# A hybrid attention and convolution layer: later weights are split on GpSimd in the middle of a pair of heads, and a row's maximum is carried from its first part into its second

## The chip, the cores and the metric

The kernel runs on one core of a Trainium2 chip. It uses TensorE (PE, matrix products and transposes), VectorE (DVE), ScalarE (ACT), GpSimd (POOL) and the DMA queue of SyncE (SP). The time is device microseconds of the whole program; smaller is better. A profile is one execution with every instruction's start and duration on record.

## The reference, cut to what matters

One layer: an RMS-normalised, modulated input goes through one projection, which feeds a convolution module and grouped-query attention; both are gated, joined and projected out. The change lies in the attention and in the preparation of weights that are used behind it.

```python
def attend_blocked(q, k, v):          # 8 query heads, 2 key heads, 1024 latent queries,
    ...                               # 1024 latent + 256 context keys
    s = jnp.einsum('bqkgd,bskd->bkgqs', qblk, k).astype(jnp.float32) * scale
    pr = jax.nn.softmax(s, axis=-1).astype(v.dtype)
    return jnp.einsum('bkgqs,bskd->bqkgd', pr, v)
...
conv = conformer_conv(...) * silu(...)            # ends in: y @ w_pw + b_pw
out = jnp.concatenate([attn, conv], axis=-1) @ w_out[l]
```

The softmax subtracts each row's maximum over all 1280 keys. The matrix products are done in two parts each (a rounded high part `hi` and the rest `lo`), so every weight and every tile of probabilities is split once: `hi` is a rounded copy, `lo` is the source less `hi`.

## The kernel before, in words

The program has three stages: the projection with the convolution (to about 306 us of the span), the attention (to about 550 us), and a tail with the layer norm, the pointwise product and the output projection.

In the attention the work comes in 32 units (group `g` of 256 queries, head `h`), taken two at a time as 16 pairs. A unit has two tiles of 128 queries (`t`) and five blocks of 256 keys (`k`). Its steps are named by two letters, the unit of the pair and the tile or block: `qa`, `qb` are the score products into PSUM (1024 keys and 256 keys); `ma`, `mb`, `mc` make the negated maximum of a row (over the first 1024 keys, over the other 256, and the smaller of both); `ex` is the exponential on ScalarE, which takes that maximum as its bias; `tr` turns a block on TensorE into one of two PSUM banks `pt`; `ra`, `hi`, `lo` split it; `pv` multiplies by the values; `rz`, `gs`, `ol`, `ad`, `gt`, `mu`, `mh`, `ml` normalise, gate and split the result. `MODE = "DRRRD"` says how a block is split: blocks 0 and 4 have `hi` on ScalarE and `lo` on VectorE, both straight from PSUM; blocks 1 to 3 are first copied to SBUF by ScalarE (`ra`), then `hi` is a VectorE cast from SBUF to SBUF (L700) and `lo` a GpSimd subtraction (L706). The bank `pt` is free again when `lo` (blocks 0, 4) or `ra` (blocks 1 to 3) has read it.

The order is written out by hand: `ORDER` gives each step a place in time, repeated every `PERIOD` = 13.4 for the 16 pairs, and every engine takes its steps in that order. Steps with a place over 13.4 run beside later pairs. Folded into one period, VectorE's order is `hi13 hi01 hi02 ma00 mb00 rz0 mc00 rz1 lo04 lo10 ma01 mb01 mc01 hi11 ad1 hi12 mu hi03 ma10 mb10 mc10 lo14 lo00 ma11 mb11 mc11 ad0`, and GpSimd's is `lo13 lo01 gs1 lo02 gs0 lo03 ml lo11 lo12`.

Other work is hung into the same order by `hooks`. Four weight tiles for the tail (`wo0`, `wo1`, `wp0`, `wp1`) are fetched by DMA (`stage`) and split a half at a time (`split`, 128x512 each), one half in each of the pairs 8 to 15, at place 0 of the pair, that is behind `ad0` and ahead of `hi13`. Before the change both parts of a split are VectorE's: a cast (L114) and a subtraction (L116). In pairs 0 to 13 `q_turn` transposes queries for later units (L609) at place 4, into a bank of the same two as `pt`.

Of the kernel before, what the change touches and what calls it, by code (L numbers as in the profile page):

```python
# [11 lines left out]
BF16 = mybir.dt.bfloat16  # L12
AF = mybir.ActivationFunctionType
ALU = mybir.AluOpType
AX = mybir.AxisListType
# [3 lines left out]
P = 128  # L19
# [5 lines left out]
KEYS = S + CTX  # L25
# [5 lines left out]


ORDER = {
# [13 lines left out]
PERIOD = 13.4  # L47
# [19 lines left out]
OA = 23.31, 25.5, 31.35  # L67

WP = 8

MODF = 3
TLO = ['dp', 'pp', 'pp', 'dd', 'dd', 'dd', 'pd', 'dd']
# [8 lines left out]
class Layer:  # L81
# [27 lines left out]
    def split(self, hi, lo, src, hi_on="act", lo_on="dve"):  # L109
        nc = self.nc  # L110
        if hi_on == "act":
            nc.scalar.activation(hi, src, AF.Copy)
        else:
            nc.vector.tensor_copy(out=hi, in_=src)  # L114
        eng = nc.gpsimd if lo_on[0] == "p" else nc.vector
        eng.tensor_sub(out=lo, in0=src, in1=hi.bitcast(F32))  # L116

# [532 lines left out]

    def op_ma(self, u, t):
        st = self.st[u]
        st["nm", t] = nm = self.small([P, 3], "nm", "nm")
        r = self.nc.vector.reduce_max(out=nm[:, 0:1], in_=self.s5[:, 1536 * t:1536 * t + 1024], axis=AX.X, negate=True)  # L654
        self.s_deps("DVE", r, [st["q", t, 0]])

    def op_mb(self, u, t):
        st = self.st[u]
        r = self.nc.vector.reduce_max(out=st["nm", t][:, 1:2], in_=self.s5[:, 1024 + 256 * t:1280 + 256 * t],  # L659
                                      axis=AX.X, negate=True)  # L660
        self.s_deps("DVE", r, [st["q", t, 1]])

    def op_mc(self, u, t):
        nm = self.st[u]["nm", t]
        self.nc.vector.tensor_tensor(out=nm[:, 2:3], in0=nm[:, 0:1], in1=nm[:, 1:2], op=ALU.min)  # L665

    def op_ex(self, u, t):
        nc, st = self.nc, self.st[u]
        if "z" not in st:
            st["z"] = self.small([P, 2], "z", "z")  # L670
        st["e", t] = e = self.e5.tile([P, KEYS], F32, tag="e", name=f"e{u[0]}{u[1]}{t}")
        ex = nc.scalar.activation(e, self.s5[:, t * KEYS:(t + 1) * KEYS], AF.Exp, bias=st["nm", t][:, 2:3],  # L672
                                  accum_out=st["z"][:, t:t + 1])
        self.s_deps("ACT", ex, [st["q", t, 0], st["q", t, 1]])
        self.s_use[t] = ex.ins

    def op_tr(self, u, k):
# [160 lines left out]
    def run(self):  # L838
# [10 lines left out]
        with ExitStack() as ctx:  # L849
# [9 lines left out]
            with ExitStack() as att:  # L859
                ps = att.enter_context(psum("ps", 1))  # L860
                self.s5 = ps.tile([P, 2 * KEYS], F32, tag="s5", name="s5")
                self.pv_bank = lambda u: pv.tile([P, 512], F32, tag="acc", name=f"pv{u[0]}{u[1]}")
                self.s_use = [None, None]
                self.sync_dep = mybir.DependencyInfo(mybir.DependencyClass.Sync, mybir.DependencyReason.DATA)
                hooks = []
                add = lambda t, fn: hooks.append((t, fn))
                acc = {}

                def proj(g, t):
                    if t == 0:  # L870
                        acc[g] = self.bank(QTAG[g], f"q1{g}")
                    self.mm_tok(acc[g], wq, g, t)
                for g in range(1, 4):
                    for t in range(2):
                        add(QP[g - 1][t], lambda g=g, t=t: proj(g, t))
                    add(QN[g - 1], lambda g=g: hl.update({(1, g): self.q(1, g, acc[g].rearrange(
                        "p (t n) -> p t n", t=2))}))
                    add(QS[g - 1], lambda g=g: hl.update({(1, g): self.q_split(1, g, hl[1, g])}))
                for i, (c, g) in enumerate(((1, 0), (0, 1), (1, 1), (0, 2), (1, 2), (0, 3), (1, 3))):
                    for hp in range(2):  # L880
                        add((2 * i + hp) * PERIOD + QT, lambda c=c, g=g, hp=hp: self.q_turn(c, g, hl[c, g], hp))
                st, wt, src = {}, {}, {"wo0": 0, "wo1": 1, "wp0": 0, "wp1": 256}

                def stage(n):
                    if n[1] == "o":
                        st[n] = self.out_stage(0, src[n])
                    else:
                        st[n] = self.w_stage(w_pw, [(src[n], 256)], n, 0)
                    wt[n] = [self.b4(list(st[n].shape), f"{n}{x}", F32R) for x in "hl"]

                def split(n, h):
                    hi, lo, x = (x.rearrange("p a b -> p (a b)")[:, 512 * h:512 * h + 512] for x in (*wt[n], st[n]))
                    self.split(hi, lo, x, hi_on="dve")
                for i, n in enumerate(src):
                    add((WP + 2 * i - 1) * PERIOD, lambda n=n: stage(n))
                    for h in range(2):
                        add((WP + 2 * i + h) * PERIOD, lambda n=n, h=h: split(n, h))
                nw = []

                def tail_pools():  # L900
                    att.close()
                    pools["acc"] = ctx.enter_context(psum("po", 4))
                    pw = ctx.enter_context(psum("pw", 1))
                    self.pw_bank = lambda g, ob: (pw, pv)[ob].tile([P, 512], F32, tag="acc", name=f"pw{g}{ob}")
                    nw.extend([wt["wo0"], wt["wo1"]])
                add(TAIL + CLOSE, tail_pools)
                steps = []
                for g in range(4):
                    steps += [lambda g=g: self.ln_stats(g, 0), lambda g=g: self.ln_stats(g, 1),
                              lambda g=g: self.ln_norm(g), lambda g=g: self.ln_swish(g)]  # L910
                for f, t in zip(steps, LN):
                    add(TAIL + t, f)
                add(TAIL + SILU, lambda: self.nc.scalar.activation(self.small([P, 1], "sj", "sj"), self.ones[:, 0:1],
                                                                   AF.Silu))
                for g, t in enumerate(OA):
                    add(TAIL + t, lambda g=g: self.out_mm(0, g, nw, 0))
                self.attention(hooks)
# [27 lines left out]
    def start(self, w_in):  # L945
# [18 lines left out]
        def scale(i):  # L964
            self.nc.vector.tensor_scalar(out=self.xs[i], in0=self.xs[i], scalar1=r.pop(i), scalar2=None, op0=ALU.mult)
        steps = {"L": self.mod_load, "X": tokens, "W": lambda h: st.update({h: self.w_stage(w_in, wcol, "wglu0", h)}),
                 "S": split, "T": self.mod_split, "C": self.mod_mm, "D": self.mod_cols,
                 "Q": lambda i: r.update({i: self.norm_stats(self.xs[i])}), "R": scale,
                 "P": self.turn_x, "Y": self.tap_rows, "V": self.taps, "U": self.make_u, "M": mm}
# [100 lines left out]
```

## Time and profile before

| | us |
|---|---|
| median of 3 runs (684.4 to 806.51) | 684.53 |
| the profiled execution | 683.55 |
| its span, first to last instruction | 681.7 |
| busy in it: PE / DVE / ACT / POOL | 650.2 / 537.4 / 352.9 / 332.5 |
| mean granted TensorE clock | 0.994 |

Busy time of an engine is the time in which an instruction of it runs. Matmul ends are modelled, so TensorE's busy time overstates its work a little. Idle time of an engine matters only where it holds up the chain that ends last.

### The profile page before, as it was taken

To read this page: it belongs to the slowest core of one execution; us is meant where nothing else is said; L and a number is where in the kernel's file an instruction comes from. 1 tells how busy PE (TensorE), PEld (TensorE's weight loads), DVE (VectorE), ACT (ScalarE), POOL (GpSimd) and SP (SyncE) were. 2 spreads that over 40 slices of the span, in tenths; PEclk is the share of its full clock that TensorE was granted. 3 is DMA by queue.
4 is the path that set the end of the run, shared out by engine and by line. 5 is a ranking of instruction groups with operands and counts; after the bars stand their busy time and mean duration, and the time that the engine had idled before them with its cause. 6 is when DMAs were issued, how large, how long until landed. Compare 5 with 4: busy or idle time off the path is not lost.

```text
span 681.7 us, 11003 instructions
## 1 busy us (share of the span) xinstructions
PE 650.2 (95%) x4258; PEld 572.3 (84%) x4258; DVE 537.4 (79%) x844; ACT 352.9 (52%) x578; POOL 332.5 (49%) x289
## 2 busy tenths in 40 slices
PE   4989999999999999997999999899999999999997
PEld 1467799888888999996899999888888878888885
DVE  2698789749999999876999999999999953545422
ACT  3564325554343122226888888788888845441000
POOL 1244804957329132885656766565566564121200
PEclk9899999999999999999999999999999999999999
DMA  8984310312653232100010001000100021133711
GB/s 266 319 225 129 116 36 1 94 31 62 217 185 124 71 101 78 32 1 1 1 32 1 1 32 60 3 32 25 40 1 1 1 93 32 62 124 132 256 60 46
DMA packets 51251, 53.28 MB, mean 78 GB/s; under 512 B 4521, under 2 KB 41697, under 8 KB 51200
## 3 DMA queue, kind: packets, MB, share of 16 engines
q1 hardware_dynamic: 51104, 52.57, 24.4%
q8 instruction: 33, 0.54, 0.3%
q14 instruction: 18, 0.15, 0.1%
q10 hardware_dynamic: 96, 0.02, 0.0%
HBM read 44.20 MB, written 8.39 MB: 77 GB/s over the span
## 4 chain that ended last, share of the span: by engine, by line
PE 67%; DVE 23%; issue 3%; DMA 3%; ACT 2%; SPq 1%; POOL 0%; DVEq 0%; ACTq 0%
PE o L820 12%; PE pv L715 8%; PE s L636 8%; PE pt L682 7%; DVE y L456 6%; PE g L386 6%; PE a L386 6%; PE kv L412 4%; DVE yp L456 4%; PE pw L531 3%; PE zc L386 3%; PE q L412 3%; DVE p L700 3%; DVE nm L654 2%; DMA wm<-in_w_mod 2%
## 5 line engine op out<-in xcount | busy, mean ns | idle before, releaser
L706 POOL TENSOR_TENSOR p<-raw,p 128x512 fp32r<-128x512 f32 x96 | 127.0, 1337 | 81.2 <-DVE p L700 70.8
L636 PE MATMUL s<-kT,qT 128*128 128x512 f32 (+1 forms) x384 | 100.8, 372 | 4.6 <-ACT e L672 4.5
L715 PE MATMUL pv<-p,v 128*128 128x256 f32 x640 | 103.2, 292 | 0.7 <-DVE mm L747 0.7
L456 DVE SCALAR_TENSOR_TENSOR yp<-up,cw,yp 128x1024 f32<-128x1024 f32 x77 | 99.1, 1287 | 1.9
L682 PE MATMUL pt<-ident,e 128*128 128x128 f32 x640 | 93.5, 273 | 1.0 <-DVE p L706 0.8
L672 ACT ACTIVATE e<-s,nm 128x1280 f32<-128x1280 f32 x64 | 85.0, 1329 | 14.3 <-DVE nm L665 14.1
L715 PEld LDWEIGHTS pv<-p,v 128*128 128x128 f32 x640 | 85.9, 189 | 4.5 <-DVE mm L747 1.5
L654 DVE TENSOR_REDUCE nm<-s 128x1 f32<-128x1024 f32 x64 | 77.7, 1214 | 0.6
L682 PEld LDWEIGHTS pt<-ident,e 128*128 128x128 f32 x640 | 73.3, 141 | 2.6 <-PE pv L715 1.2
L636 PEld LDWEIGHTS s<-kT,qT 128*128 128x128 f32 x384 | 62.7, 189 | 11.6 <-ACT e L672 5.7
L691 ACT ACTIVATE raw<-pt 128x512 f32<-128x512 f32 x96 | 57.5, 600 | 9.6 <-PE pt L682 5.5
L700 DVE CAST p<-raw 128x512 fp32r<-128x512 f32 x96 | 47.3, 520 | 1.8 <-ACT raw L691 1.2
L698 ACT ACTIVATE p<-pt 128x512 fp32r<-128x512 f32 x64 | 38.5, 602 | 11.6 <-PE pt L682 10.3
L706 DVE TENSOR_TENSOR p<-pt,p 128x512 fp32r<-128x512 f32 x64 | 40.9, 676 | 1.4 <-ACT p L698 1.4
L456 DVE SCALAR_TENSOR_TENSOR y<-up,cw,y 128x1024 f32<-128x1024 f32 x25 | 40.8, 1632 | 0.8
L833 DVE TENSOR_TENSOR r<-o,gb 128x512 f32<-128x512 f32 (+1 forms) x17 | 10.8, 656 | 30.6 <-PE o L820 30.6
L659 DVE TENSOR_REDUCE nm<-s 128x1 f32<-128x256 f32 x64 | 26.9, 421 | 9.1 <-PE s L636 7.7
L441 POOL TENSOR_TENSOR yz<-yz,ct 128x512 f32<-128x512 f32 x24 | 33.6, 1433 | 0.0
L123 POOL TENSOR_TENSOR qr<-qr,mhalf 128x8 f32<-128x8 f32 (+1 forms) x13 | 21.5, 1657 | 9.0 <-DVE qr L122 8.8
L440 ACT ACTIVATE ct<-up,cw 128x512 f32<-128x512 f32 x24 | 15.7, 713 | 12.9 <-DVE up L424 9.9
L116 POOL TENSOR_TENSOR ul<-u,uh 128x512 fp32r<-128x512 f32 x8 | 12.2, 1528 | 20.2 <-DVE uh L114 13.6
L665 DVE TENSOR_TENSOR nm<-nm 128x1 f32<-128x1 f32 x64 | 20.2, 315 | 1.7
(578 smaller groups left out, 1751.7 us busy)
## 6 DMA issues: line engine op xcount, KB each, us to landing
x<-in_x SPq DMA_DIRECT2D x8, 512.0 KB, 5.5
wg<-in_w_mod SPq DMA_DIRECT2D x8, 512.0 KB, 4.0
xr<-in_x SPq DMA_DIRECT2D x8, 512.0 KB, 8.7
out<-r SPq DMA_DIRECT2D x15, 256.0 KB, 2.0
wm<-in_w_mod SPq DMA_DIRECT2D x12, 256.0 KB, 6.7
zc_d<-zc SPq DMA_DIRECT2D x4, 512.0 KB, 3.3
za_d<-za SPq DMA_DIRECT2D x4, 512.0 KB, 4.1
zar<-za_d SPq DMA_DIRECT2D x4, 512.0 KB
```

The costliest lines, as they stand in the source:

```text
L386: nc.tensor.matmul(acc[h], lhsT=ww, rhs=uu[k][:, h * 512:(h + 1) * 512], start=first and i == 0, stop=last and i == 2)
L412: self.nc.tensor.matmul(acc[:, t * 256:(t + 1) * 256], lhsT=x, rhs=y, start=k == 0 and i == 0, stop=k == NK - 1 and i == 2)
L456: nc.vector.scalar_tensor_tensor(out=out, in0=up[:, w:w + S], scalar=cw[:, w:w + 1], in1=y if w else st["y2"], op0=ALU.mult, op1=ALU.add)
L636: mm = nc.tensor.matmul(self.s5[:, s0 + k0:s0 + k0 + n], lhsT=qt[:, h % 4, t * P:(t + 1) * P], rhs=kT[:, w, k0:k0 + n], start=w == 0, stop ...
L654: r = self.nc.vector.reduce_max(out=nm[:, 0:1], in_=self.s5[:, 1536 * t:1536 * t + 1024], axis=AX.X, negate=True)
L672: ex = nc.scalar.activation(e, self.s5[:, t * KEYS:(t + 1) * KEYS], AF.Exp, bias=st["nm", t][:, 2:3], accum_out=st["z"][:, t:t + 1])
L682: nc.tensor.transpose(out=tp[:, i * 256 + t * P:i * 256 + (t + 1) * P], in_=st["e", t][:, (2 * k + i) * P:(2 * k + i + 1) * P], identity=s ...
L691: self.nc.scalar.activation(raw, st["T", k], AF.Copy)
L700: nc.vector.tensor_copy(out=st["p", k][:, 0], in_=st["T", k])
L706: eng.tensor_sub(out=p[:, 1], in0=st["T", k], in1=p[:, 0].bitcast(F32))
L715: nc.tensor.matmul(st["pv"][:, 0:256], lhsT=self.v[:, kt, u[1] // 4].rearrange("p w d -> p (w d)"), rhs=st["p", k][:, j, i * 256:(i + 1) * ...
L820: self.nc.tensor.matmul(o, lhsT=p, rhs=q, start=half == k == i == 0, stop=half == 1 and k == 3 and i == 2)
```

## The change

It does two things. First, the eight half splits of `wo0`, `wo1`, `wp0`, `wp1` go from VectorE to GpSimd, cast and subtraction both, and from place 0 of their pair to place 7.0 (`WPS`), which on GpSimd lies behind `gs0` and ahead of `lo03`. Second, the maximum over the last 256 keys is no longer a plain reduction: `mb` becomes one `tensor_scalar` that negates the scores, takes the minimum with the value that `ma` left in column 0 (a per-row scalar operand), writes the elementwise result to a bfloat16 tile `mj` that nobody reads, and accumulates the minimum into column 1. `mc` goes away in all 64 places, and `ex` takes its bias from column 1.

```diff
-    "qa00": 0.0, "qb00": 1.04, "ma00": 2.04, "mb00": 2.2, "mc00": 2.74, "ex00": 3.76, "qa01": 3.85, "qb01": 4.53,
+    "qa00": 0.0, "qb00": 1.04, "ma00": 2.04, "mb00": 2.2, "ex00": 3.76, "qa01": 3.85, "qb01": 4.53,
...
 WP = 8
+WPS = 7.0
...
-            nc.vector.tensor_copy(out=hi, in_=src)
+            (nc.gpsimd if hi_on == "pool" else nc.vector).tensor_copy(out=hi, in_=src)
...
-        st["nm", t] = nm = self.small([P, 3], "nm", "nm")
+        st["nm", t] = nm = self.small([P, 2], "nm", "nm")
...
     def op_mb(self, u, t):
         st = self.st[u]
-        r = self.nc.vector.reduce_max(out=st["nm", t][:, 1:2], in_=self.s5[:, 1024 + 256 * t:1280 + 256 * t],
-                                      axis=AX.X, negate=True)
+        nm = st["nm", t]
+        junk = self.sm.tile([P, 256], BF16, tag="mj", name="mj", bufs=2)
+        r = self.nc.vector.tensor_scalar(out=junk, in0=self.s5[:, 1024 + 256 * t:1280 + 256 * t], scalar1=-1.0,
+                                         scalar2=nm[:, 0:1], op0=ALU.mult, op1=ALU.min, accum_out=nm[:, 1:2])
         self.s_deps("DVE", r, [st["q", t, 1]])
-
-    def op_mc(self, u, t):
-        nm = self.st[u]["nm", t]
-        self.nc.vector.tensor_tensor(out=nm[:, 2:3], in0=nm[:, 0:1], in1=nm[:, 1:2], op=ALU.min)
+        st["mb", t] = r.ins
...
-        ex = nc.scalar.activation(e, self.s5[:, t * KEYS:(t + 1) * KEYS], AF.Exp, bias=st["nm", t][:, 2:3],
+        ex = nc.scalar.activation(e, self.s5[:, t * KEYS:(t + 1) * KEYS], AF.Exp, bias=st["nm", t][:, 1:2],
...
-                    self.split(hi, lo, x, hi_on="dve")
+                    self.split(hi, lo, x, hi_on="pool", lo_on="pool")
...
-                        add((WP + 2 * i + h) * PERIOD, lambda n=n, h=h: split(n, h))
+                        add((WP + 2 * i + h) * PERIOD + WPS, lambda n=n, h=h: split(n, h))
```

Three places show how instructions stand. VectorE at the start of pair 12, before the change: `nm` are the maxima (L654 `ma`, L659 `mb`, L665 `mc`), `mm` is `ad0`, the two rows of `wp0` are the half split, the three casts of L700 are `hi13`, `hi01`, `hi02`, and L706 is `lo04`.

```order
L665 TENSOR_TENSOR nm_5485<-nm_5485 128x1
L747 TENSOR_TENSOR mm24_5505<-pv24_5410,ol24_5483 64x256
L114 CAST wp0h_5292<-wp0s0_5290 128x512
L116 TENSOR_TENSOR wp0l_5293<-wp0s0_5290,wp0h_5292 128x512
L700 CAST p253_5432<-raw253_5433 128x512
L700 CAST p261_5480<-raw261_5481 128x512
L700 CAST p262_5496<-raw262_5497 128x512
L654 TENSOR_REDUCE nm_5540<-s5_2897 128x1
L659 TENSOR_REDUCE nm_5540<-s5_2897 128x1
L722 RECIPROCAL rz_5543<-z_5348 128x2
L665 TENSOR_TENSOR nm_5540<-nm_5540 128x1
```

The same steps of pair 12 on VectorE now (L655 is `ma`, L662 the new `mb`):

```order
L662 TENSOR_SCALAR mj_5490,nm_5485<-s5_2897,nm_5485 128x256
L747 TENSOR_TENSOR mm24_5505<-pv24_5408,ol24_5483 64x256
L700 CAST p253_5432<-raw253_5433 128x512
L700 CAST p261_5480<-raw261_5481 128x512
L700 CAST p262_5497<-raw262_5498 128x512
L655 TENSOR_REDUCE nm_5538<-s5_2897 128x1
L662 TENSOR_SCALAR mj_5540,nm_5538<-s5_2897,nm_5538 128x256
L722 RECIPROCAL rz_5542<-z_5346 128x2
L722 RECIPROCAL rz_5545<-z_5255 128x2
L706 TENSOR_TENSOR p264_5547<-pt264_5521,p264_5547 128x512
```

The cast and the subtraction of the weight are gone from between `ad0` and `hi13`, and no `mc` stands between the two `rz`. GpSimd now, in the same pair, where before `gs26` was followed at once by `p263` (L732 is `gs`, L706 `lo`, L768 `ml`; the rows of `wp0` are the half split):

```order
L706 TENSOR_TENSOR p262_5497<-raw262_5498,p262_5497 128x512
L732 TENSOR_TENSOR gs26_5636<-zar2_4641,rz_5542 128x2x64
L115 CAST wp0h_5292<-wp0s0_5290 128x512
L117 TENSOR_TENSOR wp0l_5293<-wp0s0_5290,wp0h_5292 128x512
L706 TENSOR_TENSOR p263_5534<-raw263_5535,p263_5534 128x512
L768 TENSOR_TENSOR mal2_5222<-ma25_5630,mah2_5221 128x256
```

Two instructions came in between `gs0` and `lo03`; `lo03` and what follows keep their order. In the tail, which a scheduler orders, some transposes and products of TensorE and ScalarE's copies stand in a changed order as well.

## Rows read from the trace of the kernel before

**Rows 1.** The page, chain that ended last, by engine.

```profile
PE 67%; DVE 23%; issue 3%; DMA 3%; ACT 2%; SPq 1%; POOL 0%; DVEq 0%; ACTq 0%
```

**Rows 2.** Windows: from:to, us, busy of PE, PEld, DVE, ACT, POOL, clock, DMA.

```profile
339.20:411.01 71.81, 71.81 (x552) 67.67 (x551) 66.77 (x137) 63.58 (x112) 47.24 (x45) 1.00 0.06 20
411.01:534.44 123.43, 117.66 (x887) 109.19 (x886) 119.57 (x234) 101.05 (x176) 74.30 (x72) 1.00 0.06 20
...
566.00:681.67 115.67, 111.38 (x609) 96.17 (x607) 49.79 (x92) 24.96 (x42) 19.05 (x14) 0.99 0.30 105
```

**Rows 3.** Waits of PE, 427 to 519 us, then 310 to 330 us: total, times, longest.

```profile
PE qt L609 <- DVE p L706: 5.3, 6, 0.9
...
PE qt L609 <- DVE p L706: 1.1, 1, 1.1
```

**Rows 4.** Chain, 366 to 411 us (pairs without a split), by line.

```profile
by line: PE pv L715 34.0%; PE s L636 32.3%; PE pt L682 30.6%; PE qt L609 2.0%; PE gt L753 1.5%
```

**Rows 5.** Chain, 481 to 490 us (pair 12, with a split): start, length, what.

```profile
483.73 0.34 DVE wp0h L114
...
484.10 0.69 DVE wp0l L116
484.80 2.10 DVE p L700 x3
...
488.63 0.60 DVE p L706
...
489.36 0.52 PE qt L609 x4
```

**Rows 6.** Casts L700, 484 to 487 us, then 392.9 to 394.3 us: ns min/median/max.

```profile
L700 DVE CAST p<-raw x3: 422/425/1516, 484.7 to 485.4; 128x512 fp32r<-128x512 f32 x3
...
L700 DVE CAST p<-raw x3: 409/414/414, 393.1 to 393.8; 128x512 fp32r<-128x512 f32 x3
```

**Rows 7.** Timeline of POOL, pair 5, then pair 12: start, us, what, idle before.

```profile
384.13 0.40 POOL L732 TENSOR_TENSOR gs<-zar,rz 128x128 f32<-128x128 f32 x1
387.79 1.29 POOL L706 TENSOR_TENSOR p<-raw,p 128x512 fp32r<-128x512 f32 x1 [3.26 <-DVE p L700]
389.03 0.74 POOL L768 TENSOR_TENSOR mal<-ma,mah 128x256 fp32r<-128x256 f32 x1
...
485.28 2.77 POOL L706 TENSOR_TENSOR p<-raw,p 128x512 fp32r<-128x512 f32 x2 [2.47 <-DVE p L700]
```

**Rows 8.** Timeline of DVE: pair 5, then pair 0.

```profile
385.67 0.42 DVE L700 CAST p<-raw 128x512 fp32r<-128x512 f32 x1
...
387.23 0.42 DVE L700 CAST p<-raw 128x512 fp32r<-128x512 f32 x1
...
389.23 0.56 DVE L665 TENSOR_TENSOR nm<-nm 128x1 f32<-128x1 f32 x1
389.71 1.28 DVE L706 TENSOR_TENSOR p<-pt,p 128x512 fp32r<-128x512 f32 x2
...
303.92 1.00 DVE L665 TENSOR_TENSOR nm<-nm 128x1 f32<-128x1 f32 x1
...
324.79 0.90 DVE L665 TENSOR_TENSOR nm<-nm 128x1 f32<-128x1 f32 x1
```

**Rows 9.** Timeline of PE's weight loads, pair 5.

```profile
390.19 0.66 PEld L715 LDWEIGHTS pv<-p,v 128*128 128x128 f32 x4
390.79 0.46 PEld L682 LDWEIGHTS pt<-ident,e 128*128 128x128 f32 x4
```

**Rows 10.** Groups by line and shape: busy us, mean ns | idle before.

```profile
L659 DVE TENSOR_REDUCE nm<-s 128x1 f32<-128x256 f32 x58 | 24.4, 421 | 6.9 <-PE s L636 5.5
...
L672 ACT ACTIVATION_READ_ACCUMULATOR e<-s,nm 128x1 f32 x59 | 11.5, 195 | 0.0
...
L493 DVE TENSOR_SCALAR n<-n,bmv 128x512 f32<-128x512 f32 x4 | 3.1, 785 | 1.5 <-POOL bmv L123 1.5
...
L116 POOL TENSOR_TENSOR wq00l<-wq0s,wq00h 128x1024 fp32r<-128x1024 f32 x1 | 3.4, 3413 | 13.9 <-ACT wq00h L112 13.9
```

More of the change, by code (lines that the diff above doesn't have):

```diff
@@ L671, in op_ex @@
         st["e", t] = e = self.e5.tile([P, KEYS], F32, tag="e", name=f"e{u[0]}{u[1]}{t}")
-        ex = nc.scalar.activation(e, self.s5[:, t * KEYS:(t + 1) * KEYS], AF.Exp, bias=st["nm", t][:, 2:3],
+        ex = nc.scalar.activation(e, self.s5[:, t * KEYS:(t + 1) * KEYS], AF.Exp, bias=st["nm", t][:, 1:2],
                                   accum_out=st["z"][:, t:t + 1])
-        self.s_deps("ACT", ex, [st["q", t, 0], st["q", t, 1]])
+        self.s_deps("ACT", ex, [st["q", t, 0], st["q", t, 1], st["mb", t]])
         self.s_use[t] = ex.ins
```

6 rows, old and new, of the table ORDER are left out of this document.

## The prediction

> **What bounds the kernel now.** I read the page first, then windows over the pairs, then the waits and the chain inside one pair of each kind, then the timelines of VectorE and GpSimd there. The chain that ended last is 67% TensorE and 23% VectorE [rows 1], so TensorE is the bound and VectorE takes over somewhere. The windows say where [rows 2]. Their bounds are starts of the first exponential of a pair: 339.20 is pair 2, 411.01 pair 7, 534.44 pair 15. Five pairs without a split take 71.81 us, 14.36 each, and TensorE is busy for all 71.81 of it; the chain there is TensorE alone, scores, transposes and value products [rows 4]. The next eight intervals hold the eight half splits and take 123.43 us, 15.43 each. In 427 to 519 us TensorE waits for one thing only: the transposes of queries, six times, up to 0.9 us, for VectorE's `lo04`, which has to free a PSUM bank [rows 3].
>
> The chain of such a pair shows how a half split gets there [rows 5]. Behind `ad0` VectorE does the weight's cast and subtraction (0.34 and 0.69 us on the chain), then the three casts `hi13`, `hi01`, `hi02` in 2.10 us, then maxima, then `lo04`, and TensorE goes on 0.13 us after that. Three casts should not take 2.10 us: in a pair without a split they take 409 to 414 ns each, here the third takes 1516 [rows 6]. It began after GpSimd's `lo13` had started at 485.28 [rows 7], a GpSimd instruction of 1.3 us. The same is seen at `mc10`, a VectorE instruction on one column: it began at 389.23 while GpSimd's `ml` ran from 389.03 to 389.77, took 0.56 us and ended at 389.79 [rows 7, 8]. So a VectorE instruction that reads and writes SBUF alone is held while GpSimd works, and the maxima and `lo` that read PSUM are not. A split thus costs VectorE 1.03 us of its own and 1.10 us (1516 less 412) of holding, 2.13 in all, of which 1.07 (15.43 less 14.36) reaches TensorE and 1.06 is hidden.
>
> **The change part by part.**
>
> *The split leaves VectorE.* Its 1.03 us go from between `ad0` and `hi13`, which then stand as in a pair without a split, and there the third cast is not held. What is late next is TensorE itself, so no pair gets below 14.36. Eight times 14.36 is 114.9, against 123.43: **8.5 us saved**.
>
> *The split arrives on GpSimd.* Behind `gs0`, which ends at 384.53 in a pair without a split, GpSimd waits 3.26 us for `hi03` [rows 7]. The subtraction is the same shape as `lo03`: 1.29 us. A GpSimd cast is in no row. It streams one input where the subtraction streams two, so I bound it by 0.65 (half of it) and 1.29 and take 0.8, nearer to the half. That fills 384.6 to 386.8 and ends before `lo03` could start at 387.79: GpSimd's own queue (`lo03`, `ml`, `lo11`, `lo12` stand behind the split) loses nothing by it directly. But VectorE's `hi11` begins at 385.67 [rows 8], inside the subtraction. It would be held until 386.8 and end some 0.28 us later, as the 1516 ns cast ended at 486.90, 0.28 behind the first of the two instructions of 1.3 us from 485.28; that is 0.9 us late. `hi12` then finds GpSimd idle, `hi03` is 0.9 late, and so are `lo03` behind it, `ma10` and `mb10`. With a cast of 0.65 or 1.29 the hold moves between `hi11` and `hi12`, and I get 0.6 to 1.0. What catches most of it: `lo14` no longer waits for `mc10`, worth 0.45 of its 0.56 us. So `lo14` starts 0.45 late, at 390.16, and its part of the 1.28 us ends at 390.8 instead of 390.35; the transposes that need its bank load at 390.79 [rows 9]. That is 0.1 us late in each of eight pairs, **0.8 us lost** (0 with a hold of 0.6, 1.6 with one of 1.0). `lo03` would end at 390.0, ahead of the value products that load at 390.19 [rows 9]. If that cover were gone, each further 0.1 us of hold would cost 0.8 us.
>
> *`mc` goes, `mb` changes.* 64 `mc` are taken out, and 64 reductions become a `tensor_scalar` with an accumulated result. None of that kind stands in the trace. The reduction over the same 256 columns of PSUM takes 421 ns; the only `tensor_scalar` with two scalars on a big tile takes 785 for 512 columns [rows 10]. I take 0.42 to 0.5, since column count sets both, and keep 0.79 as the other end. It must now wait for `ma` to finish, where the old one could follow it directly; this is 0.1 us, as much as the wait of `mc` for `mb`. The queue behind it is the same as behind `mc`, and `ex` waits for it instead of `mc`. In pairs 1 to 6 all this lies beside TensorE's work and is worth nothing; in pairs 7 to 14 it is counted above. It is on the chain in pair 0: there `mc00` took 1.00 us from 303.92 and again 0.90 us from 324.79, held by GpSimd [rows 8]. The new `mb` reads PSUM and should not be held: 1.00 becomes some 0.55, and of 0.90 some 0.75 goes, where TensorE waited 1.1 us for the `lo04` behind it [rows 3]. **1.2 us saved**, 0 if TensorE's projection work in that pair sets the pace anyway.
>
> On accumulated results a page speaks against this edit: the Trainium skill, "VectorE: DVE Perf Modes", section "Two Vector instructions with no wait between them", says that an operation which also writes out its accumulator is two instructions. No VectorE instruction of this trace shows it; ScalarE's exponential does have such a second instruction, of 195 ns [rows 10]. By the page, with that duration as an estimate, `lo14` would come 0.2 us later in eight pairs and the sum would be 1.6 us higher.
>
> *The tail.* TensorE is busy for 111.38 of its 115.67 us [rows 2], and no work is added. The changed order there I put at 0, with 1.2 us either way.
>
> Sum: 683.55 (the profiled execution) − 8.5 + 0.8 − 1.2 = 674.6. The median of the runs is 0.98 above the profiled one, so I predict **675.6 us**, and 673.4 (no hold on `lo14`, tail 1.2 better, rounded) to 678 (pair 0 gives nothing, tail 1.2 worse) for this case itself.
>
> **The rivals.**
>
> *The third cast is held all the same.* Whether `hi02` gets in ahead of `lo13` hangs on little: `hi13` and `hi01` were some 10 ns longer where it lost [rows 6]. For: pairs are shifted by the new hold. Against: what stood ahead of `hi13` in the lost cases, the weight's subtraction, is gone. If it is held, 1.10 us plus 0.1 to 0.3 left of the middle hold meet the 1.06 that is hidden: up to 0.35 per pair, 2.8 us, 678.4.
>
> *The new `mb` is slow.* At 0.79 us `lo14` comes 0.36 later in eight pairs: 2.9 us, 678.5. For: the row of 785 ns. Against: it is for twice the columns.
>
> *Nothing is gained by moving between these two engines.* GpSimd holds VectorE for as long as VectorE's own split took, and the pairs stay at 15.43: 683.55 − 1.2 + 0.98 = 683.3. For: one held cast costs 1.10 us, as much as the split. Against: the hold falls where TensorE is ahead. The Trainium skill says this in "Perfetto Trace Analysis", section "Optimizing Scalar/DVE Operations": both share a read port, so that offloading between them might not help.
>
> *Slower: GpSimd's cast is long.* If it takes 3.4 us, the longest row of a 128x1024 subtraction there [rows 10], it ends at 388.0 and the subtraction at 389.3; `hi11` is held by the one and `hi12` by the other, and `hi03` begins near 390.2 instead of 387.23, 3.0 late. Less 0.45 for `mc10` and 0.4 of slack, TensorE loses 2.15 per pair: 17.2 − 8.5 − 1.2 = 7.5 us, 692.0. It turns slower from a hold of 2.1 us on, a cast of some 2.5. Against: nothing suggests that one input costs more than two.
>
> **How the numbers follow.** Forecast 0.60; third cast held 0.16; slow `mb` 0.09; nothing gained 0.07; long cast 0.04; better than 673 by the tail or pair 0, 0.04. The range of 673 to 681 takes in the first three, and two of them together; it leaves out 683.3, 692 and the last. What a measurement of this kernel can tell from no change is about 2%, 13.7 us: 670.8 to 698.2. All of these cases lie inside, so "same" has 0.95, faster 0.03 (all of pair 0's and the tail's waits gone too), slower 0.02 (more than the long cast gives).
>
> **What would show it.** Starts of the exponentials from pair 7 to pair 15 in 115 to 116 us; no wait of the query transposes for `lo04` in pairs 8 to 14; three casts of 0.41 us ahead of `ma00`; `hi11` held for 0.6 to 1.0 us behind the split on GpSimd; a GpSimd cast of 0.65 to 1.29 us; a `mb` of 0.42 to 0.5 us that is never held. It is wrong if the pairs stay above 15 us, if `mb` takes 0.6 us or more, or if the tail moves by more than 1.2 us.

## The result, and the profile after

The changed kernel takes **679.0 us** (median of 6 runs, 678.02 to 681.29) beside 684.61 us for the kernel before on the same chip: a ratio of 0.9916, with a 95% interval of 0.9895 to 0.9937. It is 5.6 us faster; the interval lies below 1, but the gain is less than the 2% that one such comparison is taken to tell. It lies in the forecast range of 673 to 681, though above the 673.4 to 678 that the forecast gave for its own case; 675.6 was forecast. The profiled execution took 678.08 us, its span is 676.3.

Three groups answer at once to [rows 1 to 3]. The chain that ended last, by engine, on the page of the changed kernel:

```profile
PE 76%; DVE 15%; SPq 2%; DMA 2%; issue 2%; ACT 2%; POOL 0%; DVEq 0%; ACTq 0%
```

Windows of the changed kernel (from:to, length, busy of PE, PEld, DVE, ACT, POOL, then clock, DMA share, GB/s): pair 2 to pair 7, pair 7 to pair 15, first output product to the end.

```profile
337.88:409.68 71.80, 71.80 (x551) 67.67 (x550) 62.65 (x136) 62.79 (x112) 47.08 (x46) 1.00 0.07 23
409.68:525.10 115.42, 115.28 (x877) 108.31 (x876) 102.85 (x217) 100.06 (x176) 88.19 (x87) 1.00 0.06 20
544.15:676.30 132.15, 123.81 (x673) 105.17 (x671) 55.93 (x104) 31.16 (x53) 25.65 (x21) 1.00 0.29 100
```

The last window of the kernel before, cut at its own first output product:

```profile
552.68:681.70 129.02, 122.38 (x673) 105.13 (x670) 56.54 (x104) 31.53 (x53) 25.72 (x21) 0.99 0.29 102
```

VectorE's share of the chain fell from 23% to 15%, TensorE's rose from 67% to 76%. The eight intervals from pair 7 to pair 15 take 115.42 us where they took 123.43 [rows 2], and TensorE is busy for 115.28 of it: it waits for nothing that the view of waits shows from 409.68 to 525.10, where there were six waits for `lo04` [rows 3]. But the last window grew by 3.1 us with the same 673 products, so the tail gave back more than a third of those 8.0 us.

What stands in pair 12 now, GpSimd first, then VectorE (start, length, what), beside [rows 5, 7 and 8]:

```profile
483.40 0.40 POOL L732 TENSOR_TENSOR gs<-zar,rz 128x128 f32<-128x128 f32 x1
483.75 0.61 POOL L115 CAST wp0h<-wp0s 128x512 fp32r<-128x512 f32 x1
484.44 1.28 POOL L117 TENSOR_TENSOR wp0l<-wp0s,wp0h 128x512 fp32r<-128x512 f32 x1
487.73 1.28 POOL L706 TENSOR_TENSOR p<-raw,p 128x512 fp32r<-128x512 f32 x1 [2.01 <-ACT raw L691]
```

```profile
485.14 0.87 DVE L700 CAST p<-raw 128x512 fp32r<-128x512 f32 x1
...
487.14 0.42 DVE L700 CAST p<-raw 128x512 fp32r<-128x512 f32 x1
487.47 1.22 DVE L655 TENSOR_REDUCE nm<-s 128x1 f32<-128x1024 f32 x1
488.82 0.49 DVE L662 TENSOR_SCALAR_CACHE_REDUCE mj<-s,nm 128x256 bf16<-128x256 f32 x1
489.23 1.29 DVE L706 TENSOR_TENSOR p<-pt,p 128x512 fp32r<-128x512 f32 x2
```

The split fits into the gap ahead of `lo03`. `hi11` begins at 485.14 inside its subtraction and takes 0.87 us instead of 0.42 [rows 8]: it is the one cast of the pair that is held. So it is in pairs 8 to 13 (0.84 to 0.88 us each). In pair 14, which has no query transposes, `hi11` comes earlier against the split and is held longer. All casts L700 from pair 7 to pair 15 (ns min/median/max), then `hi11` of pair 14:

```profile
L700 DVE CAST p<-raw x48: 407/415/1182, 413.0 to 522.2; 128x512 fp32r<-128x512 f32 x48
```

```profile
513.68 1.18 DVE L700 CAST p<-raw 128x512 fp32r<-128x512 f32 x1
```

From the end of `ma10` (487.47 + 1.22) to `lo14` it is 0.54 us; in pair 5 before, where `mc10` was held, it was 0.93, from the end of this `ma10` to 389.71 [rows 8]:

```profile
387.56 1.22 DVE L654 TENSOR_REDUCE nm<-s 128x1 f32<-128x1024 f32 x1
```

The costs of the new instructions over the whole run, from the groups by line and shape (ns min/median/max):

```profile
L662 DVE TENSOR_SCALAR_CACHE_REDUCE mj<-s,nm x64: 472/484/489, 303.2 to 535.2; 128x256 bf16<-128x256 f32 x64
L662 DVE DVE_READ_ACCUMULATOR mj<-s,nm x64: 78/83/86, 303.6 to 535.6; 128x1 f32 x64
```

```profile
L115 POOL CAST wp0h<-wp0s x2: 612/612/613, 483.7 to 498.2; 128x512 fp32r<-128x512 f32 x2
```

Where the time of each kernel lies is best seen in five stretches of its profiled execution, cut at the first score product `s`, at the first exponential of pairs 1, 7 and 15, and at the first output product `o`; the first stretch and the five add up to the span. All kernels of the experiments stand in the table, so that it is given once. One bound needs care: in the kernel before and in e7 all eight half splits lie between pair 7 and pair 15, in all others the eighth lies behind pair 15's first exponential, in the next column.

| us | to first `s` | `s` to pair 1 | pair 1 to 7 | pair 7 to 15 | pair 15 to `o` | `o` to end | span |
|---|---|---|---|---|---|---|---|
| before | 298.50 | 27.21 | 85.28 | 123.44 | 18.22 | 129.01 | 681.7 |
| after | 298.47 | 25.91 | 85.30 | 115.43 | 19.05 | 132.14 | 676.3 |
| e1, last split later | 298.61 | 25.78 | 85.29 | 115.44 | 19.11 | 129.45 | 673.7 |
| e2, splits at 4.5 | 299.40 | 25.34 | 85.28 | 114.58 | 18.59 | 129.37 | 672.6 |
| e3, splits at 9.0 | 300.75 | 25.35 | 85.29 | 116.47 | 19.36 | 129.44 | 676.7 |
| e9, e3 once more | 299.46 | 25.54 | 85.26 | 119.71 | 19.35 | 129.42 | 678.8 |
| e4, subtraction three times | 298.56 | 25.89 | 85.30 | 127.29 | 18.74 | 133.21 | 689.0 |
| e5, split alone | 298.72 | 27.18 | 85.29 | 118.45 | 19.13 | 131.04 | 679.8 |
| e8, split alone at 4.5 | 298.50 | 27.20 | 85.31 | 115.38 | 19.01 | 133.39 | 678.8 |
| e6, maxima alone | 299.66 | 25.33 | 85.28 | 123.22 | 19.28 | 129.03 | 681.8 |
| e7, maxima alone, tail of after | 298.67 | 25.96 | 85.30 | 124.18 | 18.20 | 131.75 | 684.1 |

After minus before: −1.3 in pair 0, −8.0 in the split pairs, +0.8 ahead of the first output product, +3.1 behind it: −5.4 in all, as the spans say. Since the eighth half changed its column, the −8.0 and the +0.8 belong together: from pair 7 to `o`, where every kernel has all eight, it is 141.66 us before and 134.48 after, **−7.2**. The question that the forecast left is the 3.1.

### The profile page after: what moved, and what is told of

Its sections match the earlier page's. It is cut to its first block, busy times and chain, and to the rows that moved or that the text cites. A ratio compares the mean times of both kernels' runs of the same rounds, so it can differ in the third digit from the quotient of the medians.

```text
span 676.3 us, 11074 instructions
## 1 busy us (share of the span) xinstructions
PE 651.2 (96%) x4258; PEld 574.2 (85%) x4258; DVE 513.0 (76%) x828; ACT 350.3 (52%) x578; POOL 348.2 (51%) x305
## 4 chain that ended last, share of the span: by engine, by line
PE 76%; DVE 15%; SPq 2%; DMA 2%; issue 2%; ACT 2%; POOL 0%; DVEq 0%; ACTq 0%
PE o L820 12%; PE pv L715 11%; PE s L637 10%; PE pt L682 10%; DVE y L457 6%; PE g L387 6%; PE a L387 6%; PE kv L413 4%; DVE yp L457 4%; PE q L413 4%; PE pw L532 3%; PE zc L387 3%; DMA wm<-in_w_mod 2%; PE mrow L265 2%; SPq L216 1%
## 5 line engine op out<-in xcount | busy, mean ns | idle before, releaser
L706 POOL TENSOR_TENSOR p<-raw,p 128x512 fp32r<-128x512 f32 x96 | 128.3, 1352 | 64.0 <-DVE p L700 42.2
L655 DVE TENSOR_REDUCE nm<-s 128x1 f32<-128x1024 f32 x64 | 78.1, 1221 | 5.6 <-PE s L637 4.9
L662 DVE TENSOR_SCALAR_CACHE_REDUCE mj<-s,nm 128x256 bf16<-128x256 f32 x64 | 30.9, 483 | 20.1 <-PE s L637 18.0
L700 DVE CAST p<-raw 128x512 fp32r<-128x512 f32 x96 | 42.6, 470 | 1.7 <-ACT raw L691 1.2
L706 DVE TENSOR_TENSOR p<-pt,p 128x512 fp32r<-128x512 f32 x64 | 41.2, 682 | 1.6 <-ACT p L698 1.6
L265 PE MATMUL mrow<-wm,sc 128*2 128x256 f32 x48 | 16.1, 511 | 4.3 <-ACT sc L162 3.5
```

Source lines behind the costliest of these rows:

```text
L700: nc.vector.tensor_copy(out=st["p", k][:, 0], in_=st["T", k])
L706: eng.tensor_sub(out=p[:, 1], in0=st["T", k], in1=p[:, 0].bitcast(F32))
```

## The experiments

**The tail: order, or GpSimd?** In the tail a scheduler orders what stands behind the last hook, and the place of the last half split changes that order. e1 moves the last half alone behind `lo03` of pair 15; TensorE's last 700 instructions then stand in the order of the kernel before.

```diff
-  add((WP + 2 * i + h) * PERIOD + WPS, lambda n=n, h=h: split(n, h))
+  add((WP + 2 * i + h) * PERIOD + (9.0 if 2 * i + h == 7 else WPS), lambda n=n, h=h: split(n, h))
```

> The changed kernel, with the last of the eight half splits one GpSimd instruction later (behind lo03 of pair 15 instead of ahead of it). With that the scheduler puts TensorE's tail into exactly the order of the kernel before. Theory A, the tail's changed order costs the 3 us that are missing (behind the first output product the changed kernel takes 132.1 us, the kernel before 129.0): the tail is back at 129 us and the whole at 676.0 (675 to 677). Theory B, it is the last split's work beside pair 15, or the clock: the tail stays near 132 and the whole at 679. Pairs 7 to 14 stay at 14.43 us by both.

Measured: 676.58 us (675.47 to 678.14), ratio 0.9878 [0.9834, 0.9922]. From `o` to the end it is 129.45 us; the split pairs are as in the changed kernel. The chain shows where much of the 2.7 us was. First the changed kernel from 600 to 625 us (start, length, what):

```profile
608.58 0.23 PE nt L510 x2
...
608.84 0.26 ACT s L512
...
609.30 0.56 ACT s L512
609.86 0.53 ACT sh L113
...
610.47 0.70 DVE sl L117
...
611.21 6.00 PE pw L532 x46
```

Then e1, at the same products:

```profile
600.81 0.22 PE nt L510 x2
601.03 7.51 PE o L820 x33
608.54 5.99 PE pw L532 x48
```

The transposes `nt` feed ScalarE's `s` and `sh` and VectorE's `sl`, and the products `pw` need both. In e1, 33 output products stand between the last `nt` and its `pw` and cover that chain of some 2.4 us (from 608.82 to 611.21). In the changed kernel only four do, which TensorE's timeline shows and the chain does not; the last of them, then the first `pw`:

```profile
609.56 0.39 PE L820 MATMUL o<-wo03h,mcl 128*128 128x512 f32 x1
610.43 0.39 PE L532 MATMUL pw<-sh,wp0h 128*128 128x256 f32 x1 [0.48 <-ACT sh L113]
610.65 0.28 PE L532 MATMUL pw<-sh,wp1h 128*128 128x256 f32 x1
611.21 0.38 PE L532 MATMUL pw<-sl,wp0h 128*128 128x256 f32 x1 [0.28 <-DVE sl L117]
```

So TensorE is idle there for 0.48 and 0.28 us. Before, the chain was covered as in e1. Two shorter gaps (567.72 to 568.22, behind VectorE's `ma`, and 593.97 to 594.81, behind `sl`) stand in the changed kernel's chain and not in e1's; TensorE is idle 0.30 and 0.29 us in them. Together that is 1.35 us, and in the whole tail TensorE is idle for 1.3 us more than in e1 (132.15 less 123.81, against 129.47 less 122.41). The other 1.4 us count as busy time; the ends of matmuls are modelled, and what of it is waiting is not shown.

e7 is the other side of it: the maxima changed, the splits left on VectorE in their old place, and the tail's instructions of TensorE in the changed kernel's order. e6 is its pair, with the last half at 6.0, which gives the order of before (the diff is e6's; in e7 all eight halves have place 0).

```diff
-                    self.split(hi, lo, x, hi_on="pool", lo_on="pool")
+                    self.split(hi, lo, x, hi_on="dve")
...
-  add((WP + 2 * i + h) * PERIOD + WPS, lambda n=n, h=h: split(n, h))
+  add((WP + 2 * i + h) * PERIOD + (6.0 if 2 * i + h == 7 else 0), lambda n=n, h=h: split(n, h))
```

> Only the maxima are changed; the splits stay on VectorE in their old place, but for the last half, which comes a little later so that TensorE's order in the tail is that of before. Theory A: the third cast of a split pair is held by GpSimd as before (1.5 us), the pairs stay at 15.4 to 15.5, 123 to 124 us from pair 7 to pair 15, and the gain is that of pair 0 alone, 1.3 us from the first score product to pair 1: about 683.3 us. Theory B (the accumulated maximum brings a good part of the gain by itself, since it leaves out one instruction that GpSimd may hold): pairs below 15, total 680 us or less.

> The maxima are changed and the splits stay on VectorE in their old place, all of them; TensorE's instructions of the tail then stand in the order of the changed kernel. Theory A (the tail's order costs the 3 us that the changed kernel lost there): from the first output product to the end 132 us instead of 129 to 129.5, about 686.3 us, 3 above the same kernel with the order of before. Theory B (the 3 us came with GpSimd's split in pair 15, whatever TensorE's order): 129 to 129.5 us in the tail, about 683.3 us.

Measured: e6 683.46 us (ratio 0.9971 [0.995, 0.9992]), e7 686.37 us (1.002 [1.0003, 1.0037]); from `o` to the end 129.03 and 131.75 us. None of the eight halves is split on GpSimd in either, so the order of the tail alone costs 2.7 us, and the rival theory falls. e6 also says what the maxima are worth without the move: pair 0, and nothing in the split pairs (142.50 us from pair 7 to `o`, 142.38 in e7, 141.66 before), where the third cast is still held, as this row of casts L700 from 484 to 503 us shows (ns min/median/max; compare [rows 6]):

```profile
L700 DVE CAST p<-raw x9: 418/422/1512, 484.3 to 500.5; 128x512 fp32r<-128x512 f32 x9
```

**The split alone.** e5 has GpSimd's split at its place and the old maxima, with e1's tail (one product of TensorE stands a little later). Against e1 its edit puts back `nm` with three columns, `reduce_max`, `op_mc` and the `mc` entries of `ORDER` (cut).

```diff
-        st["nm", t] = nm = self.small([P, 2], "nm", "nm")
+        st["nm", t] = nm = self.small([P, 3], "nm", "nm")
...
-        r = self.nc.vector.tensor_scalar(out=junk, ...
+        r = self.nc.vector.reduce_max(out=st["nm", t][:, 1:2], ...
...
+        self.nc.vector.tensor_tensor(out=nm[:, 2:3], in0=nm[:, 0:1], in1=nm[:, 1:2], op=ALU.min)
```

> The split of the later weights goes to GpSimd into the middle of the pair, as in the changed kernel; the maxima stay as before (reduction and mc). The last half's split stands behind lo03 of pair 15, so that TensorE's order in the tail is that of before. Theory A (each part works where it was costed): mc10 of a split pair is held by GpSimd's lo13 as in a pair without a split (0.56 us instead of 0.16), lo14 behind it comes some 0.4 to 0.5 us late on top of the 0.07 of the middle hold, the pairs last 14.8 to 15.0, 118.5 to 120 us from pair 7 to pair 15; pair 0 gives nothing; about 681 us. Theory B (the maxima are worth nothing in the split pairs, TensorE hides them): pairs of 14.4 to 14.5, 115.5 us, only pair 0's 1.3 us missing against the kernel with the same tail and both parts (676.6): about 678 us.

Measured: 682.3 us (680.04 to 683.11), ratio 0.9958 [0.9944, 0.9973]. The pairs from 8 to 14 last 14.82 to 14.89 us, theory A's size, and pair 0 gives nothing (27.18). VectorE's timeline in e5, pair 12, then GpSimd's:

```profile
488.30 0.96 DVE L666 TENSOR_TENSOR nm<-nm 128x1 f32<-128x1 f32 x1
489.18 0.41 DVE L701 CAST p<-raw 128x512 fp32r<-128x512 f32 x1
...
492.65 0.66 DVE L666 TENSOR_TENSOR nm<-nm 128x1 f32<-128x1 f32 x1
493.24 1.27 DVE L707 TENSOR_TENSOR p<-pt,p 128x512 fp32r<-128x512 f32 x2
```

```profile
487.95 1.29 POOL L117 TENSOR_TENSOR wp0l<-wp0s,wp0h 128x512 fp32r<-128x512 f32 x1
...
492.56 0.73 POOL L769 TENSOR_TENSOR mal<-ma,mah 128x256 fp32r<-128x256 f32 x1
```

Here two `mc` of a pair are held: `mc01` by the split's subtraction, and `mc10` by `ml` (`mal`). `hi11`, behind `mc01`, is not (0.41 us). Theory A had only named `mc10`; and the only waits of TensorE from 410 to 536 us that the view shows are not for `lo14` but for `ad1` (L748), which comes behind the held `mc01` and `hi11`:

```profile
PE pv L716 <- DVE mm L748: 2.1, 7, 0.6
```

So the size was right and its place only in part. An `mc` that is not held takes 0.16 us (before, pair 5, 385.59), so `mc01` was held 0.80 us here, where the changed kernel's `hi11` is held 0.45. The total is 1.3 above the 681 expected; the profiled tail, 131.04 us, holds ten microseconds at a lower granted clock that e1's has not:

```profile
559.64:569.64 10.00, 8.88 (x48) 8.14 (x49) 4.93 (x12) 6.07 (x10) 5.20 (x5) 0.83 0.17 54
```

A mean of 0.83 over 10 us, part of it at 1.2 instead of 2.4 GHz, is 1.7 us of full speed lost, about as much as e5's tail is longer than e1's (1.6). e8 asks whether the maxima are worth those 0.4 us per pair wherever the split lies: e5 with the split at 4.5, between `gs1` and `lo02`, and TensorE's tail in the changed kernel's order.

```diff
-WPS = 7.0
+WPS = 4.5
```

> The maxima as before (reduction and mc), the split on GpSimd at 4.5, between gs1 and lo02, where GpSimd's split meets no mc of VectorE; TensorE's tail stands in the order of the changed kernel. Theory A (the accumulated maximum is worth something in a split pair only where GpSimd's work of the split falls on an mc, as on mc01 at place 7.0): pairs of 14.36 to 14.5, some 115 us from pair 7 to pair 15; pair 0 as before (27.2 us from the first score product to pair 1); the tail 132 us from the first output product; about 680 us. Theory B (it is worth 0.4 us in every split pair, wherever the split lies): pairs of 14.8 or more, 118 us, about 683 us.

Measured: 680.94 us, ratio 0.9939 [0.9921, 0.9958]; 115.38 us from pair 7 to pair 15, pairs of 14.36 to 14.60. Theory A held: with the split there, the old maxima cost 0.8 us in this stretch (e2, below, has the same place and the new maxima: 114.58), not 0.4 in every pair. Two pairs, 10 and 12, stand out with 14.60 and 14.55 us: there GpSimd's `gs` caught a cast as well. VectorE in pair 12, `mc01` and the second cast of the middle:

```profile
486.38 0.44 DVE L666 TENSOR_TENSOR nm<-nm 128x1 f32<-128x1 f32 x1
...
487.62 0.61 DVE L701 CAST p<-raw 128x512 fp32r<-128x512 f32 x1
```

Held are 0.28 and 0.19 us, and 0.19 is lost (14.55 less 14.36), so these pairs too cover some 0.3 us of hold, with every `mc` in place. Its tail of 133.39 us is a further instance of the slower order, with a mean granted clock of 0.98 in it where the changed kernel's was 1.00.

**Where the split lies.** e2 and e3 are the changed kernel with one number changed: 4.5, and 9.0, behind `lo03` and ahead of `ml`. Both have TensorE's tail in the order of before (in e2 one product stands a little later). The diff is e2's.

```diff
-WPS = 7.0
+WPS = 4.5
```

> The changed kernel, with all eight half splits earlier on GpSimd, between gs1 and lo02. The tail's TensorE order is that of the kernel before. Theory A, a split costs only by the VectorE cast that it holds: here the split itself ends before hi11 starts and lo02 behind it overlaps hi11 by 0.3 us or less, so the pairs go from 14.43 to 14.36 to 14.38 us, and the whole to 675.3 (674.5 to 676.3). Theory B, the 0.07 us per pair come from GpSimd's longer queue: they stay, 675.9 or more.

> The changed kernel, with all eight half splits later on GpSimd, between lo03 and ml; the tail's TensorE order is that of the kernel before. No VectorE cast runs beside the split itself, but ml, lo11 and lo12 come 1.9 us later, and lo12 then overlaps hi13, the first of the three casts ahead of ma00. Theory A, what counts is which cast is held and how much slack stands behind it: hi13 is held for 0.8 to 1.2 us, of which some 1.1 us is hidden, so the pairs take 14.4 to 14.7 us and the whole 676 to 678; if hi02 is caught as well, 15.4 us and 683. Theory B, only the split itself holds anything: 14.36 us and 675.3.

Measured: e2 **674.46 us** (674.36 to 674.98), ratio 0.9841 [0.9806, 0.9877], the fastest of all. Its pairs last 14.36 us, TensorE's own time. In its pair 12 GpSimd's split ends at 484.01 and VectorE's three casts of the middle, from 485.21 on, take 0.42 to 0.43 us each: the split meets VectorE where it is busy with instructions that read PSUM, or idle. Theory A held. GpSimd, then VectorE:

```profile
482.03 0.61 POOL L115 CAST wp0h<-wp0s 128x512 fp32r<-128x512 f32 x1
482.72 1.29 POOL L117 TENSOR_TENSOR wp0l<-wp0s,wp0h 128x512 fp32r<-128x512 f32 x1
```

```profile
483.25 1.22 DVE L655 TENSOR_REDUCE nm<-s 128x1 f32<-128x1024 f32 x1 [0.49 <-PE s L637]
...
485.21 0.43 DVE L700 CAST p<-raw 128x512 fp32r<-128x512 f32 x1
```

e3 took 680.31 us (678.44 to 685.22), ratio 0.9935 [0.9908, 0.9962], 2 to 4 us more than theory A expected. Most of its split pairs last 14.4 to 14.5 us, but the interval from pair 9 to pair 10 took 16.08. The casts L700 there, 448 to 457 us, and GpSimd's timeline:

```profile
L700 DVE CAST p<-raw x3: 410/1501/1561, 451.1 to 453.0; 128x512 fp32r<-128x512 f32 x3
```

```profile
447.73 1.30 POOL L117 TENSOR_TENSOR wo0l<-wo00s,wo0h 128x512 fp32r<-128x512 f32 x1
448.98 0.73 POOL L768 TENSOR_TENSOR mal<-ma,mah 128x256 fp32r<-128x256 f32 x1
449.67 2.75 POOL L706 TENSOR_TENSOR p<-raw,p 128x512 fp32r<-128x512 f32 x2
452.84 2.78 POOL L706 TENSOR_TENSOR p<-raw,p 128x512 fp32r<-128x512 f32 x2 [0.42 <-DVE p L700]
```

The split, ahead of `ml`, `lo11` and `lo12`, makes these late, and two of the three casts behind `ad0` were caught by one GpSimd instruction each. This is the forecast's rival of the third cast, in another place. e9 is the same kernel, run once more.

> The kernel with the split at 9.0, once more, unchanged, for the pair that lasted 16.08 us. Theory A (whether VectorE's second and third cast get in ahead of GpSimd's lo12 is decided by a margin that differs from run to run): other pairs, or another number of them, are long this time. Theory B (it follows from the weight or the pair): the interval from pair 9 to pair 10 is 16.1 us again and no other above 14.6.

Measured: 680.56 us (one run). Now the intervals from pairs 8, 9, 11 and 12 last 15.92, 15.62, 16.06 and 15.60 us, and the one from pair 10 only 14.05. Theory A held: which pairs are caught differs between two executions of one kernel. It would fit the scatter of e3's times, but only these two executions were traced.

**How much hold the pairs bear.** e4 does the subtraction of the first seven half splits three times, which adds 2 x 1.3 us to GpSimd and changes no value; the last half, left as it is, stands at 9.0, and with that the tail is in the changed kernel's order here.

```diff
+                    for _ in range(0 if (n, h) == ("wp1", 1) else 2):
+                        self.nc.gpsimd.tensor_sub(out=lo, in0=x, in1=hi.bitcast(F32))
...
-  add((WP + 2 * i + h) * PERIOD + WPS, lambda n=n, h=h: split(n, h))
+  add((WP + 2 * i + h) * PERIOD + (9.0 if 2 * i + h == 7 else WPS), lambda n=n, h=h: split(n, h))
```

> The changed kernel, with the subtraction of seven of the eight half splits done three times on GpSimd, to the same output; the tail is ordered as in the changed kernel. Theory A, GpSimd's work holds the casts hi11, hi12 and hi03: the hold grows from 0.45 us to between 1.7 and 2.6, 0.5 us of that is hidden, and the seven pairs take 15.5 to 16.5 us: 687 to 694. Theory B, only GpSimd's own queue matters: it has 2.0 us to spare ahead of lo03 and lo03 another 1.1 ahead of its products, so the pairs stay at 14.4 to 14.6 us and the whole at 679 to 680.

Measured: 690.62 us (689.12 to 691.56), ratio 1.0078 [1.0051, 1.0104], slower than the kernel before and of theory A's size. The pairs from 9 to 13 last 16.27 us. In pair 12 all three casts of the middle are held now, and of the three ahead of the next `ma00`, which take 2.19 us together, the third is held as well (VectorE's timeline of e4):

```profile
491.95 1.46 DVE L700 CAST p<-raw 128x512 fp32r<-128x512 f32 x1
...
493.88 0.96 DVE L700 CAST p<-raw 128x512 fp32r<-128x512 f32 x1
...
495.09 1.16 DVE L700 CAST p<-raw 128x512 fp32r<-128x512 f32 x1
...
501.20 2.19 DVE L700 CAST p<-raw 128x512 fp32r<-128x512 f32 x3
```

TensorE's longest waits there (424 to 537 us) are again for `ad1`, then for a `lo` of VectorE:

```profile
PE pv L715 <- DVE mm L747: 2.1, 5, 0.4
PE pt L682 <- DVE p L706: 1.9, 6, 0.3
```

The three of the middle are held for 2.3 us together, the one behind them for 1.1, and 1.91 (16.27 less 14.36) reaches TensorE; e4 does not tell the two places apart. The changed kernel does, where `hi11` alone is held: in pairs 9 to 12 it is 0.45 us, and 0.07 arrives; in pair 14 it is 0.77, and 0.40 arrives (14.41, against 14.01 in e2 and e3, where 0.26 and less is held). If what is not covered is lost in full, the cover in the middle of a pair is 0.37 to 0.38 us by both.

## Why the prediction was right, and where it was off

- **Split off VectorE, −8.5, and onto GpSimd, +0.8.** Net −7.7 forecast, −7.2 measured over all eight halves. The mechanism is as put: TensorE is the bound in the split pairs, and the third cast is not held. e2, where the split's place leaves at most 0.26 us of hold, has 133.17 us from pair 7 to `o`, 8.5 less than before: the first term is right. The changed kernel's 134.48 makes the second 1.3. The hold falls on `hi11` as forecast. In pairs 8 to 13 it is 0.45 us, not 0.6 to 1.0, because GpSimd's cast takes 0.612 us, under the lower bound of 0.65, and `hi11` begins later against `gs0` (1.34 us behind its end, for 1.14 in pair 5 before); 0.07 per pair arrives, instead of 0.1. In pair 14, and behind pair 15, it is 0.8 us, and some 0.4 arrives each time (14.41 for 14.01, 19.05 for 18.59), which a figure for one pair times eight could not show.
- **What catches the hold: right in size, not in its path.** The forecast had `lo14` late and the missing `mc10`, worth 0.45 us, as what catches it. With `mc` back (e5) the pairs are 14.87, 0.43 longer, 3.0 us over the seven. But there it is `mc01` that is held, 0.35 us longer than the changed kernel's `hi11`, and TensorE waits for `ad1`, not for `lo14`. With `mc` in place some 0.3 us of hold is covered all the same (0.80 held and 0.51 lost in e5, about as much in e8), against 0.37 without. So most of the 0.43 comes from `mc01` standing in the split's way; that it equals the forecast's 0.45 is luck. Without the move (e6, e7) the maxima are worth nothing in these pairs, and with the split elsewhere (e8) 0.8 us in all.
- **`mb` with an accumulated result.** 0.42 to 0.5 us taken, 0.484 measured, and never held (472 to 489). The Trainium skill's statement in "VectorE: DVE Perf Modes", section "Two Vector instructions with no wait between them", that an operation which also writes out its accumulator is two instructions, is borne out by the DVE_READ_ACCUMULATOR rows; the second takes 0.083 us, where the estimate from ScalarE's had 0.195, and the 1.6 us that hung on it did not come.
- **Pair 0, −1.2.** Measured −1.3 in the profiled execution, and −1.9 in e2, e3 and e6; e5 and e8, with the old maxima, give 0, so the maxima are the cause. What separates the two sizes is the granted clock. In the changed kernel it is 0.93 from 310 to 320 us and 0.83 from 320 to 326; in e2, e3 and e6 it is 1.00 in both, and the stretch takes 25.33 to 25.35 us. In all five kernels in which it fell there, the changed kernel and e1, e4, e7, e9, it takes 25.54 to 25.96. e3 and e9 are one program, and it fell in e9 alone, so the order of instructions does not decide it. TensorE was busy for all of 300 to 310 us in the changed kernel and in e2 alike, and why the clock fell is not settled.
- **The tail, 0 with 1.2 either way: the step that failed.** It was +3.1, and "if the tail moves by more than 1.2 us" was one of the forecast's own signs of being wrong. The forecast took "no work is added" for "no time is added". The 673 products did stay; of the 3.1 us, 1.7 are idle time of TensorE (132.15 less 123.81, for 129.02 less 122.38), and 1.4 are busy time, as between e7 and e6 (123.81 and 122.42), whose part in it was not traced further. The order of the products was the cover for a chain of ScalarE and VectorE, and the change took much of it away, in one place above all. e1 and e7 show it from both sides. With before's order in the tail the kernel takes 676.58, 1.0 above the forecast.
- **The number and the rivals.** 679.0 is nearest to the two rivals at 678.4 and 678.5, and the range took it in only because it had been widened for them. The trace shows that neither came true: the third cast is not held in the changed kernel's split pairs, and `mb` is not slow. The third cast is caught at 9.0 (e3, e9) and in e4. A long cast did not come; e4 turned slower as that rival had it, by more GpSimd work instead. That nothing is gained by the move does not hold: the split pairs last 14.4 us, not 15.4. The forecast's lower end, 673.4, is 673.6 by its own terms.

## What to carry to other kernels

Before costing a move between VectorE and GpSimd, list in time what the one does while the other works: the same split cost 0, 0.07 or up to 1.7 us per pair, by where it met VectorE alone. When a scheduler reorders a stretch, a term of "no work added" is not 0: look in the new order for a producer whose consumer now stands close behind it, and price the chain between them. A sum of parts measured one at a time can mislead: here the maxima were worth 0.4 us per pair only together with the split's place at 7.0. And a stretch cut at fixed marks must hold the same work in both kernels: here an eighth of the moved work had crossed the mark.

## What was not expected of the hardware

- GpSimd's cast of 128x512 takes 611 to 613 ns (8 of them), less than half of its subtraction of the same shape (1.28).
- A held VectorE cast ends some 0.28 us after GpSimd's instruction: 486.01 after 485.72 in the changed kernel, the same as the 0.28 of the kernel before. The Trainium skill, "SBUF — State Buffer", section "SBUF: two separate sides", describes the port that the two share as an exclusive lock, which whichever starts first keeps for its whole instruction while the other is blocked. The rows agree in that no held cast ends ahead of GpSimd's instruction: in e3 the one of 1.56 us, from 451.13, ends 0.28 us after GpSimd's pair from 449.67. But a cast that began only then would end some 0.41 us behind it.
- The granted clock differs between executions of nearly the same program, at the start too: the first `s` comes at 298.5 to 300.75 us, and in e3 the clock is 0.83 from 50 to 60 us, where e1, e2 and e4 have 1.00.
